# RMS norms of a two-layer encoder: column sums over dealt tokens, GpSimd's power for the inverse root, and gate rows spread by DMA

## The chip, the cores and the metric

One core of one Trainium2 chip runs the whole program in a single launch. The metric is the device time of that launch in microseconds (us), the median of the runs shown; less is better. The engines are PE (matrix products; PEld is its weight load), DVE (vector), ACT (scalar), POOL (GpSimd) and SP (here only a DMA queue). Engines run side by side and wait for each other by semaphores; each works through its own queue in order.

## The reference

A trunk of two layers on one sequence of 512 tokens, width 1024, all in float32:

```python
xn = rms_norm(x, mix_norm[layer])
# layer 0: 8 heads of forgetting attention | 4 heads of differential attention
d_out = rms_norm(d_out, subln) * 0.8            # per head and token, over 128 channels
# layer 1: mLSTM, 4 heads, 256 channels each
h = num / max(abs(den), exp(-m_t))
h = rms_norm(h, head_norm) * sigmoid(og)        # per head and token, over 256 channels
x = x + mixed @ w_out
x = x + memory_cross_attention(rms_norm(x, xattn_norm), rms_norm(mem, mem_norm), wq, wkv, wo)
x = x + conv_ffn(rms_norm(x, ffn_norm), ...)
# after both layers
return rms_norm(x, final_norm)
```

`rms_norm` is `x * rsqrt(mean(x*x) + 1e-6) * gain`. So the program needs an inverse root per token (512 numbers) in these places: the first norm of each layer, the norm ahead of each cross-attention and each FFN, the norm of the memory (256 tokens), one norm for each of the 4 differential heads and each of the 4 mLSTM heads, and the last norm.

## The kernel before, in words

**Layout.** Activations lie with channels on partitions and tokens along the free dimension: `x[k]` is 128 channels by 512 tokens, eight of them. A norm thus has to sum squares across partitions, which PE does, and has to bring the inverse root, a number per token, to all partitions, since the projections are left unnormed and each result is multiplied by `rb` (128 x 512, all rows alike) when it leaves PSUM. Every float32 operand of a projection is split in a high part (ACT copy) and a low part (DVE subtraction), and PE makes three products of them (`mm3`, L340 to L342).

**Two ways to norm.** `p_norm` (L420) sums by columns: `rsqrt_cols` (L531) makes 4 products, each with a 128-token block of the squares as weights and two columns of ones as the moving operand, so that token t of block j stands in partition t, column j. `rsqrt` (L539) then takes the inverse root of this 128 x 4 tile with 12 small DVE instructions (a first guess by integer arithmetic and three Newton steps). `bcast_cols` (L554) turns the numbers back into rows: split in two parts, each part multiplied on DVE with an identity into a 128 x 512 matrix (`sqt`), each of which PE sums with a matrix of ones (L571); the sum of the two is `rb`, in PSUM or copied to SBUF by ACT. The products of `bcast_cols` are issued at once behind its DVE work. `p_row_norm` (L433) sums by rows: the squares are split (ACT and DVE), PE multiplies both parts with ones (L470), ACT copies one row to SBUF, a DMA on ACT's queue turns the row into a 128 x 4 tile `z`, POOL takes the power -0.5 (L482), one DMA on POOL's queue writes it to DRAM (`roots`, L484) and another reads it back into all 128 partitions (L489). Its last step is tied, by `nc.vector.follow()`, behind the DVE instruction issued before it.

**Who uses which.** `p_row_norm` serves the four differential heads (tile `hrb`) and the norm ahead of each cross-attention (`x_row_norm`). `p_norm` serves the start of layer 1, the memory's norm and the four mLSTM heads, which multiply straight from PSUM (`scaled`, in `mix1`), so that a PSUM bank of the pair "s" stays taken until then. Layer 0's first norm (`inverse`, `spread` in `mix0`) and the FFN's (`root`, `spread` in `ffn_steps`) are written out, and `finish` calls `rsqrt_cols` for each half of the tokens.

**mLSTM gates.** `gates` (in `mix1`) makes rows of 4 heads x 512 tokens: `mx`, a running maximum, and `mt`. `split_rows` puts their parts in a 128 x 512 tile. For each head `most` and `emts` bring one row to all partitions: DVE makes a selector, PE multiplies (L733), and ACT copies `mxb` or takes exp(-mt) into `emt`. POOL masks `mxb` into `mk` (L1721) four times for each head, ACT takes its exponential, and DVE multiplies the scores with it.

**What orders the work.** In `mix0`, `mix1` and `xattn` a planner (`Plan`, L84) emits the steps. Each has a priority, dependencies, resources (two "s" banks, two "w" banks, four accumulators, three weight slots), a duration on PE and a `chain`: the time that other engines need until its result is ready ("A", "D", "G" for ACT, DVE, POOL; "-" for a plain delay such as a DMA). The planner keeps a clock of its own and takes the first step that would be ready at it; a step whose result is thought to be later is emitted later. The engines' queues then follow what was emitted, with shifts that the tile framework makes where no order is fixed. The FFN has a second planner (`Sched`) with its own costs for each engine; there the order on DVE and ACT is as planned.

Of the kernel before, what the change touches and what calls it, by code (L numbers as in the profile page):

```python
# [16 lines left out]
P = 128  # L17
# [13 lines left out]
ROW_DMA, SPREAD_DMA = 2.7, 6.0  # L31
# [257 lines left out]
class Builder:  # L289
# [130 lines left out]
    def p_norm(self, pl, state, n, done, scale, eps, fin, deps=(), prio=None, after=0.0, fdeps=(), chain=(("A", 0.5),)):  # L420
# [12 lines left out]
    def p_row_norm(self, pl, state, scale, eps, to, fin, deps=(), prio=None, fdeps=(), chain=()):  # L433

        nc, sp = self.nc, self.sp
        st = {}

        def parts():
            st["p"] = self.row_parts(state["sq"])

        def sums():
            st["row"] = self.row_sums(st["p"], scale, eps)

        def turned():
            st["z"] = self.row_turned(st["row"])

        def spread():
            st["rb"] = self.row_spread(st["d"], to)

        a = pl.add(parts, 0, deps, prio, chain=(("A", 0.52), ("D", 0.6)))  # L450
        a = pl.add(sums, 0.43, [a], prio, take=("s",), free=("s",), chain=(("A", 0.5),))
        a = pl.add(turned, 0, [a], prio, chain=(("-", ROW_DMA),))
        a = pl.add(lambda: st.update(d=self.row_root(st["z"])), 0, [a], prio, chain=(("G", 1.05), ("-", ROW_DMA)))
        a = pl.add(spread, 0, [a], prio, chain=(("-", SPREAD_DMA),))
# [7 lines left out]
    def row_parts(self, sq):  # L462
        hi, lo = (self.til(self.sp, "sqt", dtype=F32R) for _ in range(2))
        self.split(hi[:], lo[:], sq[:])
        return hi, lo

    def row_sums(self, parts, scale, eps):
        ps = self.bank("b")
        for i, part in enumerate(parts):
            self.nc.tensor.matmul(banked(ps[:]), self.onesr[:], alternate(part[:]), start=i == 0, stop=i == 1)  # L470
        row = self.til(self.sp, "sqt")
        self.nc.scalar.activation(folded(row[0:1, :]), restored(ps[0:1, :]), AF.Copy, scale=float(scale), bias=float(eps))
        return row

    def row_turned(self, row):
        z = self.til(self.sp, "z", (P, 4))
        self.nc.scalar.dma_start(z[:], row[0:1, :].rearrange("o (p j) -> o p j", j=4))
        return z

    def row_root(self, z):  # L480
        y = self.til(self.sp, "y", (P, 4))
        self.nc.gpsimd.tensor_tensor(out=y[:], in0=z[:], in1=self.power[:], op=ALU.pow)  # L482
        d = self.til(self.dp, "roots", (1, SEQ))
        self.nc.gpsimd.dma_start(d[:].rearrange("o (p j) -> (o p) j", j=4), y[:])  # L484
        return d

    def row_spread(self, d, to):
        rb = self.til(*to)
        self.nc.gpsimd.dma_start(rb[:], d[0:1, :].to_broadcast([P, SEQ]))  # L489
        return rb  # L490

# [5 lines left out]

    def rb_to(self):
# [1483 lines left out]
```

## Time and profile before

| what | value |
|---|---|
| median of 3 runs (lowest, highest) | 1439.73 us (1436.8, 1440.22) |
| the profiled execution | 1440.03 us, its span 1438.3 us |
| PE, PEld busy | 1411.4 us (98%), 1261.0 us (88%) |
| DVE, ACT, POOL busy | 1163.3, 817.1, 81.3 us |
| chain that ended last | PE 75%, DVE 13%, ACT 4%, DMA 4%, issue 4%, POOL 1% |
| layer 0: mixer, cross-attention, FFN | about 0 to 260, 260 to 400, 400 to 735 us |
| layer 1: mixer, cross-attention, FFN with the last norm | about 735 to 955, 955 to 1100, 1100 to 1438 us |

How to read it: the span is the time from the first to the last instruction of the profiled execution, and the run's time is a little longer. Busy time of PE is the union of its matmuls as the profile models them. A dense product of 512 columns starts every 0.21 to 0.22 us, though its record is 0.38 us long, so PE can be "busy" and still start less often than it could. In a timeline the columns are start, duration, engine, line, operation, tile written, tiles read and count; a bracket gives the idle time of that engine just before, and what ended it.

### The profile page before, as it was taken

Reading aid. Unit: us, or ns where it says so; the run is one execution under the profiler, and the core shown is the slowest. Engines: PE = TensorE matmul, PEld = TensorE weight load, DVE = VectorE, ACT = ScalarE, POOL = GpSimd, SP = SyncE. Lnnn points to the kernel's source line nnn. Section 1 sums busy time; section 2 is a strip of 40 time slices with the busy share of each in tenths; the row PEclk is TensorE's granted clock in tenths of the full one; section 3 lists DMA queues with packets and bytes.
Section 4 is the critical chain, followed back from the end, with each engine's and each line's share of the span. In section 5 each row is a group of like instructions: output and inputs, shape, how many; then the busy total and the mean of one; then the engine's idle time right before and its main releaser. Section 6 shows DMA issues by size and latency. Waiting matters only on the chain.

```text
span 1438.3 us, 22036 instructions
## 1 busy us (share of the span) xinstructions
PE 1411.4 (98%) x8304; PEld 1261.0 (88%) x8304; DVE 1163.3 (81%) x2084; ACT 817.1 (57%) x1407; POOL 81.3 (6%) x129
## 2 busy tenths in 40 slices
PE   9999799999999999999999999999999999999998
PEld 7888688889888999999888788788988899999987
DVE  7777796566689999999778858657567999999985
ACT  7777574444465556565546635444445666656654
POOL 0002230000000000000000100000000000000000
PEclk9999999999999999999999999999999999999999
DMA  5232433423237666652232222333324656555412
GB/s 202 89 96 89 118 98 131 125 88 132 87 111 205 172 159 169 162 147 78 81 103 88 90 86 90 101 105 112 129 75 134 178 161 161 165 154 169 125 60 80
DMA packets 63498, 176.36 MB, mean 123 GB/s; under 512 B 8056, under 2 KB 8056, under 8 KB 63392
## 3 DMA queue, kind: packets, MB, share of 16 engines
q1 hardware_dynamic: 55344, 152.69, 32.1%
q0 software_dynamic: 6176, 21.14, 8.1%
q8 instruction: 65, 1.06, 0.3%
q10 hardware_dynamic: 1872, 1.13, 0.3%
q14 instruction: 41, 0.34, 0.1%
HBM read 172.80 MB, written 2.13 MB: 122 GB/s over the span
## 4 chain that ended last, share of the span: by engine, by line
PE 75%; DVE 13%; ACT 4%; DMA 4%; issue 4%; POOL 1%; DVEq 0%; SPq 0%; ACTq 0%; POOLq 0%
PE acc L340 15%; PE acc L341 15%; PE acc L342 15%; PE w L342 5%; PE w L341 5%; PE w L340 5%; DVE wl L262 3%; PE s L340 2%; PE s L342 2%; PE s L341 2%; PE acc L402 2%; DVE c L262 1%; PE acc L404 1%; PE acc L403 1%; DVE x L262 1%
## 5 line engine op out<-in xcount | busy, mean ns | idle before, releaser
L262 ACT CAST wh<-raw 128x1024 fp32r<-128x1024 f32 (+2 forms) x200 | 204.2, 1023 | 200.6 <-PE acc L341 112.9
L340 PE MATMUL acc<-xh,wh 128*128 128x512 f32 (+1 forms) x824 | 289.1, 351 | 1.3 <-DVE tmp L262 1.3
L342 PE MATMUL acc<-xh,wl 128*128 128x512 f32 (+1 forms) x824 | 285.0, 346 | 0.7 <-DVE wl L262 0.7
L341 PE MATMUL acc<-xl,wh 128*128 128x512 f32 (+1 forms) x824 | 285.0, 346 | 0.0
L262 DVE TENSOR_TENSOR wl<-raw,wh 128x1024 fp32r<-128x1024 f32 (+2 forms) x200 | 238.9, 1195 | 50.2 <-ACT wh L262 49.0
L340 PEld LDWEIGHTS acc<-xh,wh 128*128 128x128 f32 x824 | 156.7, 190 | 16.5 <-issue 2.3
L342 PEld LDWEIGHTS acc<-xh,wl 128*128 128x128 f32 x824 | 156.5, 190 | 16.4 <-DVE wl L262 1.5
L341 PEld LDWEIGHTS acc<-xl,wh 128*128 128x128 f32 x824 | 156.7, 190 | 14.5 <-issue 0.2
L262 DVE SCALAR_TENSOR_TENSOR c<-hs,vec,c 128x512 f32<-128x512 f32 x176 | 131.6, 748 | 3.5 <-ACT c L262 0.6
L342 PE MATMUL w<-ah,wl 128*128 128x512 f32 x304 | 115.4, 380 | 0.2
L340 PE MATMUL w<-ah,wh 128*128 128x512 f32 x304 | 115.4, 380 | 0.0
L341 PE MATMUL w<-al,wh 128*128 128x512 f32 x304 | 115.2, 379 | 0.0
L262 ACT ACTIVATE c<-hs,vec 128x512 f32<-128x512 f32 x88 | 71.0, 810 | 26.7 <-DVE hs L262 22.5
L262 ACT CAST ah<-c 128x512 fp32r<-128x512 f32 x44 | 27.3, 620 | 89.4 <-DVE c L262 89.4
L262 DVE TENSOR_TENSOR x<-acc,x 128x512 f32<-128x512 f32 (+1 forms) x43 | 28.1, 654 | 52.6 <-PE acc L342 52.5
L342 PEld LDWEIGHTS w<-ah,wl 128*128 128x128 f32 x304 | 57.5, 189 | 9.1 <-DVE wl L262 1.0
L341 PEld LDWEIGHTS w<-al,wh 128*128 128x128 f32 x304 | 57.6, 190 | 6.6
L340 PEld LDWEIGHTS w<-ah,wh 128*128 128x128 f32 x304 | 57.6, 190 | 6.5
L340 PE MATMUL acc<-mem,wh 128*128 128x256 f32 (+1 forms) x192 | 60.7, 316 | 0.0
L342 PE MATMUL acc<-mem,wl 128*128 128x256 f32 (+1 forms) x192 | 59.9, 312 | 0.0
L341 PE MATMUL acc<-mem,wh 128*128 128x256 f32 (+1 forms) x192 | 59.6, 310 | 0.0
L1483 POOL DMA_DIRECT2D sa<-in_up_dram x33 | 28.5, 863 | 513.8 <-DVE sa L262 134.1
(357 smaller groups left out, 3729.4 us busy)
## 6 DMA issues: line engine op xcount, KB each, us to landing
raw<-in_up_dram SPq DMA_DIRECT2D x55, 512.0 KB, 3.3
sa<-in_up_dram SPq DMA_DIRECT2D x33, 512.0 KB, 4.5
sa<-in_up_dram POOLq DMA_DIRECT2D x33, 512.0 KB, 5.4
dr<-in_down_dram SPq DMA_DIRECT2D x64, 256.0 KB, 3.8
ra<-in_up_dram SPq DMA_DIRECT2D x33, 256.0 KB, 4.0
raw<-in_xk_dram SPq DMA_DIRECT2D x16, 512.0 KB, 3.3
raw<-in_wo_dram SPq DMA_DIRECT2D x16, 512.0 KB, 3.2
raw<-in_xq_dram SPq DMA_DIRECT2D x16, 512.0 KB, 3.2
```

The lines of the kernel that those rows point to most:

```text
L262: i = issue(*a, **k)
L340: mm(out, wh, xh, start=first, stop=False, skip_group_check=parts)
L341: mm(out, wh, xl, start=False, stop=False, skip_group_check=parts)
L342: mm(out, wl, xh, start=False, stop=last, skip_group_check=parts)
L402: mm(ps, xh[k][:, ts], wh, start=(k == 0), stop=False)
L403: mm(ps, xh[k][:, ts], wl, start=False, stop=False)
L404: mm(ps, xl[k][:, ts], wh, start=False, stop=(k == 7))
L1483: return add("POOL", 0.0029 * cols, lambda: nc.gpsimd.dma_start(out(), src(), accum_op=ALU.add), deps, due, (), (), 6.0)
```

## The change

Five parts.

1. **The root.** `rsqrt` takes the power -0.5 on GpSimd, one instruction, in place of 11 of its 12 DVE instructions. This holds for every norm that goes through it, the last one too.
2. **The way back.** `bcast_cols` is cut in two: `diag_cols` (split and the two DVE matrices) and `spread_cols` (the two products and the copy to SBUF). They are steps of their own in the plan, with the DVE time between them told to the planner; the same in layer 0's first norm and in the FFN's `Sched`.
3. **Far norms.** `p_row_norm` goes. `p_far_norm` serves the four differential heads and mLSTM heads 0 to 2: `rsqrt_cols`, the power on GpSimd, a write to DRAM and a read to all partitions, both DMAs on POOL's queue. The planner is told `LATE` = 12.0 us for the last DMA in place of 6.0. So that the 128 x 4 tile goes to DRAM in one piece, the squares are written dealt: `by_fours` writes token 4p+j to column 128j+p. mLSTM head 3 keeps the way over PE, by way of a tile `hrb`.
4. **Cross-attention.** Its norm goes by `p_norm`; the `follow` in `query` goes too.
5. **Gate rows.** exp(-mt) is taken once, on the rows of all heads; `mx` and exp(-mt) are written to DRAM by two DMAs, and heads 1 to 3 read their row of each to all partitions by DMA (`both`), once the queries of the head before have been evacuated; `mxb` and `emt` have two buffers in place of one. Head 0 keeps `most` and `emts`.

```diff
-ROW_DMA, SPREAD_DMA = 2.7, 6.0
+ROW_DMA, SPREAD_DMA, LATE = 2.7, 6.0, 12.0
...
         def two():
-            fin(st["r"], self.bcast_cols(st["r"], n, *done))
-
-        a = pl.add(one, 0.4 * n / 512, deps, prio, take=("s",), free=("s",), chain=(("D", 2.3),), after=after)
-        return pl.add(two, 0.5 * n / 512, [a, *fdeps], prio, take=("s",), free=("s",), chain=chain)
+            fin(st["r"], self.spread_cols(st["d"], n, *done))
+
+        a = pl.add(one, 0.9 * n / 512, deps, prio, take=("s",), free=("s",), chain=(("D", 0.1), ("G", 1.05)), after=after)
+        b = pl.add(lambda: st.update(d=self.diag_cols(st["r"], n)), 0, [a], prio, chain=(("D", 0.2 + 1.2 * n / 512),))
+        return pl.add(two, 0.43 * n / 512, [b], prio, take=("s",), free=("s",), chain=(("A", 0.5),))
+
+    def by_fours(self, to, v, **k):
+
+        self.nc.scalar.activation(to.rearrange("p (j t) -> p t j", j=4), v.rearrange("p (t j) -> p t j", j=4), AF.Square, **k)
...
+    def p_far_norm(self, pl, state, scale, eps, to, fin, deps=(), prio=None, fdeps=(), chain=(), late=None):
...
         def sums():
-            st["row"] = self.row_sums(st["p"], scale, eps)
+            st["y"] = self.rsqrt_cols(state["sq"], SEQ, scale, eps)
+
+        def away():
+            st["d"] = self.til(self.dp, "roots", (1, SEQ))
+            nc.gpsimd.dma_start(st["d"][:].rearrange("o (p j) -> (o p) j", j=4), st["y"])
 
         def spread():
-            st["rb"] = self.row_spread(st["d"], to)
+            st["rb"] = self.til(*to)
+            nc.gpsimd.dma_start(st["rb"][:], st["d"][0:1, :].to_broadcast([P, SEQ]))
+
+        a = pl.add(sums, 0.45, deps, prio, take=("s",), free=("s",), chain=(("D", 0.1), ("G", 1.05)))
+        a = pl.add(away, 0, [a], prio, chain=(("-", ROW_DMA),))
+        a = pl.add(spread, 0, [a], prio, chain=(("-", late or SPREAD_DMA),))
 
         def last():
             nc.vector.follow()
...
         nc.vector.tensor_scalar(out=z, in0=ps[:, 0 : 2 * nt : 2], scalar1=float(scale), scalar2=float(eps), op0=ALU.mult, op1=ALU.add)
-        nc.vector.tensor_scalar(out=y.bitcast(I32), in0=z.bitcast(I32), scalar1=-0.5, scalar2=1597463007.0, op0=ALU.mult, op1=ALU.add)
-        nc.vector.tensor_scalar(out=zh, in0=z, scalar1=-0.5, scalar2=None, op0=ALU.mult)
-        for _ in range(3):
-            nc.vector.tensor_tensor(out=a, in0=y, in1=y, op=ALU.mult)
-            nc.vector.tensor_tensor(out=a, in0=a, in1=zh, op=ALU.mult)
-            nc.vector.scalar_tensor_tensor(out=y, in0=a, scalar=1.5, in1=y, op0=ALU.add, op1=ALU.mult)
+        nc.gpsimd.tensor_tensor(out=y, in0=z, in1=self.power[:, :nt], op=ALU.pow)
         return y
...
                     nc.scalar.copy(o["o"][:], ps[:])
-                    nc.scalar.activation(sq["sq"][:], o["o"][:], AF.Square)
+                    self.by_fours(sq["sq"][:], o["o"][:])
...
-                f = self.p_row_norm(pl, sq, 1.0 / P, EPS, (mp, "hrb", (P, SEQ), F32, 1), scaled, [w], p + SOFT_PRIO, chain=(("D", 0.66),))
+                f = self.p_far_norm(pl, sq, 1.0 / P, EPS, (mp, "hrb", (P, SEQ), F32, 1), scaled, [w], p + SOFT_PRIO, chain=(("D", 0.66),), late=LATE)
...
-            norm = self.x_row_norm(pl, 0, self.xdone[7])
+            norm = self.x_norm(pl, 0, deps=self.xdone[7])
...
                 gt["rows"] = self.split_rows(mp, mx, mt)
+                nc.scalar.activation(mt, mt, AF.Exp, scale=-1.0)
                 gt["u"] = zi
+                gt["d"] = [self.til(self.dp, n, (H, SEQ), bufs=1) for n in ("mx", "emt")]
+                for d, v in zip(gt["d"], (mx, mt)):
+                    nc.gpsimd.dma_start(d[:], v)
...
+                def both(h=h, st=st):
+                    for i, n in enumerate(("mxb", "emt")):
+                        st[n] = self.til(mp, n, bufs=2)
+                        self.spread_row(gt["d"][i], h, st[n])
+
+                if h == 0:
+                    b1 = pl.add(most, MM, [uc, qe], p, take=("s",), free=("s",), chain=(("A", 0.5),))
+                    b2 = pl.add(emts, MM, [uc, qe], p + 1, take=("s",), free=("s",), chain=(("A", 0.5),))
+                else:
+                    b1 = b2 = pl.add(both, 0, [uc, gk, *turn[-1:]], p, chain=(("-", SPREAD_DMA),))
+                turn.append(qe)
...
-                f = self.p_norm(pl, st, SEQ, (), 1.0 / 256, 0.0, scaled, ns, p + 3, fdeps=oe, chain=(("D", 1.32),))
+                if h < 3:
+                    f = self.p_far_norm(pl, st, 1.0 / 256, 0.0, (mp, "hrb", (P, SEQ), F32, 1), scaled, ns, p + 3, fdeps=oe, chain=(("D", 1.32),), late=LATE)
+                else:
+                    f = self.p_norm(pl, st, SEQ, (mp, "hrb", 1), 1.0 / 256, 0.0, lambda r, rb, st=st: st.update(rb=rb), ns, p + 3)
+                    f = pl.add(lambda scaled=scaled, st=st: scaled(st["rb"]), 0, [f, *oe], p + 3, chain=(("D", 1.32),))
```

More of the change, by code (lines that the diff above doesn't have):

```diff
@@ L460, in p_row_norm @@
         return pl.add(last, 0, [a, *fdeps], prio, chain=chain)
[L462 to L490, printed above, removed]
     def x_norm(self, pl, prio=0, after=0.0, deps=()):
@@ L561, in bcast_cols @@
         self.sub(rl, r, rh)
-        ps = self.bank("b")
-        for i, part in enumerate((rh, rl)):
+        out = []
+        for part in (rh, rl):
             dg = self.til(self.sp, "sqt", dtype=F32R)[:].rearrange("p (a b) -> p a b", b=P)
@@ L570, in bcast_cols, with spread_cols @@
             )
-            nc.tensor.matmul(banked(ps[:, :n]), self.onesr[:], alternate(dg[:, :nt, :].rearrange("p a b -> p (a b)")), start=i == 0, stop=i == 1)
-        if pool is None:
-            return restored(ps[:, :n])
+            out.append(dg[:, :nt, :].rearrange("p a b -> p (a b)"))
+        return out
+    def spread_cols(self, diags, n, pool, tag, bufs=2):
+        ps = self.bank("b")
+        for i, dg in enumerate(diags):
+            self.nc.tensor.matmul(banked(ps[:, :n]), self.onesr[:], alternate(dg), start=i == 0, stop=i == 1)
         out = self.til(pool, tag, (P, n), bufs=bufs)
-        nc.scalar.copy(folded(out[:, :n]), restored(ps[:, :n]))
+        self.nc.scalar.copy(folded(out[:, :n]), restored(ps[:, :n]))
         return out
```

83 lines of the change are left out of this document (36 added, 47 removed).

## The prediction

> **What bounds the kernel now.** First the page's busy times, then stretches of equal kind, then what PE waits for.
>
> ```profile
> PE 1411.4 (98%) x8304; PEld 1261.0 (88%) x8304; DVE 1163.3 (81%) x2084; ACT 817.1 (57%) x1407; POOL 81.3 (6%) x129
> ```
>
> PE is idle for 1438.3 - 1411.4 = 26.9 us of the span. Everything else has room, so only two things move the end: PE's own work, and the moments in which PE waits.
>
> ```profile
> 150.00:180.00 30.00, 22.47 (x110) 17.79 (x110) 22.46 (x59) 16.37 (x33) 8.99 (x14) 0.96 0.45 123
> 300.00:400.00 100.00, 100.00 (x550) 89.82 (x549) 64.41 (x113) 47.00 (x87) 0.14 (x2) 1.00 0.30 102
> 800.00:960.00 160.00, 158.71 (x777) 134.63 (x777) 113.00 (x211) 75.64 (x112) 7.21 (x11) 1.00 0.27 93
> ```
>
> These rows of busy time by stretch give length, PE, PEld, DVE, ACT, POOL, then the granted clock. A dense stretch (300 to 400) has no idle PE; the mLSTM stretch (800 to 960) has 1.3 us. The 30 us around 165 have 7.5 us, and there the granted clock falls to 0.96. So the mLSTM part can gain little by waits, only by work; layer 0's attention can gain by waits. PE's waits over the whole span, in total, times and longest:
>
> ```profile
> PE w L1047 <- ACT pt L262: 4.6, 1, 4.6
> PE s L793 <- ACT sqt L262: 3.0, 1, 3.0
> PE s L571 <- DVE sqt L262: 2.0, 5, 0.9
> ...
> PE acc L340 <- DVE tmp L262: 1.3, 2, 0.8
> ...
> PE acc L342 <- DVE wl L262: 0.7, 2, 0.4
> ```
>
> All five lie at norms. The first two are 7.5 us of the 26.9, and both belong to the last differential head:
>
> ```profile
> 152.49 0.62 ACT L262 CAST sqt<-tb 128x512 fp32r<-128x512 f32 x1
> 157.99 0.59 PE L470 MATMUL s<-sqt,ones 128*128 128x512 f32 x2
> 161.67 0.59 ACT L262 ACTIVATE sqt<-s 1x512 f32<-1x512 f32 x1
> 162.31 0.38 PE L793 MATMUL s<-ka,qa 128*128 128x256 f32 x1 [2.97 <-ACT sqt L262]
> 169.81 0.54 POOL L489 DMA_DIRECT2D hrb<-roots  x1 [2.86 <-DMA roots<-y]
> 175.00 0.75 DVE L262 SCALAR_TENSOR_TENSOR ta<-ta,warm,hrb 128x512 f32<-128x512 f32 x1 [4.49 <-DMA hrb<-roots]
> 177.78 2.61 PE L1047 MATMUL w<-pt,v 128*64 128x512 f32 x8 [4.56 <-ACT pt L262]
> ```
>
> Read it downwards. The row sum is made at 157.99, but ACT, which is behind, copies it only at 161.67; until then an "s" bank is taken and the next scores wait 2.97 us. The row then goes through three DMAs. DVE has reached the multiplication with `hrb` in its queue and stands there for 4.49 us; ACT and the transposed weights `pt` stand behind it, and PE waits 4.56 us. The planner thought the rows would be there: its chain (1.1 + 0.9 + 2.7 + 1.1 + 2.7 + 6.0) is about 15 us, while from the split at 152.49 to 175.00 it took 22.5.
>
> **The change, part by part.** What PE pays for the two ways to sum:
>
> ```profile
> 265.37 0.59 PE L470 MATMUL s<-sqt,ones 128*128 128x512 f32 x2
> 265.80 0.38 PE L340 MATMUL acc<-xh,wh 128*128 128x512 f32 x1
> 266.02 0.38 PE L341 MATMUL acc<-xl,wh 128*128 128x512 f32 x1
> ...
> 802.86 0.95 PE L536 MATMUL s<-ones,hsq 128*128 128x2 f32 x8
> 803.67 0.46 PE L340 MATMUL acc<-xh,wh 128*128 128x512 f32 x1
> ```
>
> From start to start, two products over 512 columns take 265.80 - 265.37 = 0.43 us (0.22 each), and the column sums, eight short records with eight weight loads, 803.67 - 802.86 = 0.81.
>
> *Work of PE.* Each differential head changes row sums for column sums: 4 x (0.81 - 0.43) = +1.5. Each cross-attention norm does that and adds the two products of `spread_cols`: 2 x 0.81 = +1.6. mLSTM heads 0 to 2 lose those two products: -3 x 0.43 = -1.3. Gate rows of heads 1 to 3 lose the products of L733, two a head: -6 x 0.22 = -1.3. Together +0.5 us: as work the change is neutral.
>
> *Waits at the differential heads.* The split, the row's copy on ACT and the turning DMA go; DVE frees the bank with one instruction of 0.16 us (`z`, quoted below) instead of ACT with 0.59. So the 2.97 us go by construction, unless DVE is as late as ACT was. For the second wait the real time from the sums to `hrb` is to be compared with the planned one. Landing times and the power:
>
> ```profile
> hrb<-roots POOLq DMA_DIRECT2D x4, 256.0 KB, 4.2
> ...
> roots<-y POOLq DMA_DIRECT2D x6, 2.0 KB, 2.7
> ```
>
> ```profile
> L482 POOL TENSOR_TENSOR y<-z,power x6: 1035/1294/2126, 112.5 to 965.5; 128x4 f32<-128x4 f32 x6
> ```
>
> 0.8 (sums) + 0.2 + 1.3 (power) + 0.3 + 2.7 + 4.2 is about 9.5 us; the plan now assumes 0.45 + 0.1 + 1.05 + 2.7 + 12.0, some 16.5. DVE should meet `hrb` with up to 7 us in hand, where it was 4.5 short. Of the 7.5 us I take 6.0: without them DVE's 22.46 us of work in that stretch would have 22.5 us, so something smaller on DVE will be late next. Bounds: 0 (rival B) and 7.5. The clock comes back with it: 30 us at 0.96 cost at most 1.2; I take 0.5.
>
> *Cross-attention.* The norm came by DMA and was the last thing to arrive:
>
> ```profile
> 279.89 0.69 DVE L262 SCALAR_TENSOR_TENSOR tmp<-acc,rb 128x512 f32<-128x512 f32 x1 [5.10 <-DMA rb<-roots]
> 280.72 0.45 PE L340 MATMUL acc<-xh,wh 128*128 128x512 f32 x1 [0.51 <-DVE tmp L262]
> ```
>
> PE had filled most of the gap with keys and values, so DVE's 5.10 us of waiting cost PE only 0.51 here; over both layers 1.3 (`tmp`) and 0.7 (`wl`, the split queued behind it). By PE the rows are there some 5 us after the sums. Of these 2.0 I take 1.5, bounds 0 and 2.0, against +1.6 of work: nothing is won.
>
> *The other norms.* PE's five waits at L571 (2.0 us) come from products queued right behind their DVE work. Now that work is a planned step and PE has others in between; I take 1.6, since the last mLSTM head has little else left. The root itself, where nothing covers it, at the very end:
>
> ```profile
> 1430.14 0.16 DVE L262 TENSOR_SCALAR z<-s 128x2 f32<-128x2 f32 x1 [0.76 <-PE s L536]
> ...
> 1432.36 1.27 ACT L262 ACTIVATE th<-acc,y 128x512 f32<-128x512 f32 x2 [1.06 <-DVE y L262]
> ```
>
> From the end of `z` (1430.30) to ACT's start 2.06 us; with the power at its least (1.04, DVE having nothing else) and 0.3 to hand over, 1.35: -0.7. With the longest power (2.13) it would be +0.4.
>
> Such a long one stands here:
>
> ```profile
> 117.27 1.23 DVE L262 TENSOR_TENSOR wl<-raw,wh 128x1024 fp32r<-128x1024 f32 x1 [0.78 <-ACT wh L262]
> 117.27 2.13 POOL L482 TENSOR_TENSOR y<-z,power 128x4 f32<-128x4 f32 x1 [0.36 <-ACT wh L262]
> ```
>
> The power took 1.09 us longer than the least while DVE ran 1.23. The Trainium skill, SBUF — State Buffer, "Who interferes with whom", states that GpSimd shares a port pair with DVE as an exclusive lock: a DVE instruction with two SBUF inputs and a GpSimd one that reads SBUF don't overlap, and the second to start waits for the whole of the first. This row agrees; by that rule every power beside a busy DVE is a long one and the roots save no time against 2 us of Newton steps, which would put the sum at about 1431.
>
> *The rows of the mLSTM gates, and what the trace doesn't show.*
>
> ```profile
> 25.30 0.59 ACT L262 COPY rb<-s 128x512 f32<-128x512 f32 x1
> ...
> 104.03 0.63 ACT L262 ACTIVATE tb<-ta 128x512 f32<-128x512 f32 x1
> 114.33 0.60 POOL L484 DMA_DIRECT2D roots<-y  x1 [0.30 <-POOL y L482]
> ...
> 765.67 1.28 ACT L262 ACT_TABLE_LOAD   x1
> 770.91 0.56 ACT L262 COPY mxb<-s 128x512 f32<-128x512 f32 x1
> ```
>
> ACT is spared two copies of about 0.6 us a head, DVE two selectors; added are one exponential on four rows, two DMAs of one-off rows, and six spreads of the `hrb` kind (4.2 us to land), asked for a head ahead. Hidden by PE's projections unless POOL holds them up (rival C). The dealt write of `by_fours` is not in the trace. The plain Square (`tb`) takes 0.63; thirteen of them (4 + 3 x 3), at nothing more or at double, are 0 to 8.2 us of ACT, which is 57% busy, so 0 to +4 on the path. I take 0, since the `rb` copies, rearranged on both sides, take no longer than a Square. A moved table load is bounded by one more of 1.28; I take 0.
>
> **Sum** against the profiled execution, 1440.03: work +0.5; differential waits -6.0; clock -0.5; cross-attention -1.5; L571 -1.6; the end -0.7. That is -9.8, so 1430.2. The median of the runs lies 0.3 below that execution: **1430.0 us**.
>
> **The rivals.**
>
> *B: the waits at the differential heads stay* (chance 0.16). The column sums keep the squares' tile `tb` until PE reads it, and the fox heads' masks need the same two buffers; and a POOL that waits for `roots` (2.86 us above) still holds their masks. For it: DVE, 75% busy there with the stall in it, has no slack without it. Against: 7 us in hand. Then 6.5 us of the gain fail: 1436.5.
>
> *C: slower, by POOL's queue in the mLSTM heads* (chance 0.12). A far head puts on POOL a power (1.0 to 2.1), a write (0.6), a wait for its landing (2.2 to 2.9) and a read (0.55), 4.5 to 6.2 us in order; a gate-row read can also wait there, for a buffer of the head before last. The masks of the next head queue behind. Before, masks come this long after the sums:
>
> ```profile
> 816.28 3.08 POOL L1721 TENSOR_SCALAR_AFFINE_SELECT mk<-mxb 128x512 f32<-128x512 f32 x2 [3.46 <-ACT mxb L262]
> 825.34 0.95 PE L536 MATMUL s<-ones,hsq 128*128 128x2 f32 x8
> 841.07 1.66 POOL L1721 TENSOR_SCALAR_AFFINE_SELECT mk<-mxb 128x256 f32<-128x256 f32 x2 [19.92 <-ACT wh L262]
> 859.91 0.95 PE L536 MATMUL s<-ones,hsq 128*128 128x2 f32 x8
> 872.75 1.25 POOL L1721 TENSOR_SCALAR_AFFINE_SELECT mk<-mxb 128x512 f32<-128x512 f32 x2 [3.90 <-ACT mxb L262]
> ```
>
> 13.4 us (802.86 to 816.28), 15.7 and 12.8: more than twice 6.2, which speaks against it. It decides if masks come due within about 6 us of the sums. With three heads at some 5 us, 1430 + 15 = 1445; it is slower than before from two heads on.
>
> *D: more goes than I count* (chance 0.10). DVE loses 11 small instructions at every root and ACT two 0.6 us steps at seven heads; if smaller waits in layer 0 go too and all 7.5 are won: 7.5 + 1.2 + 2.0 + 2.0 + 0.7 - 0.5, and 3 more: 1424.
>
> **How the numbers follow.** The forecast has 0.62, its own range is 1426 to 1434 (the stated bounds of waits and roots). Leaving out C and the lower part of D, 1423.5 to 1438.5 holds about 0.8. A measurement of this kernel tells about 0.3% from no change, 4.3 us, so "faster" is below 1435.4: forecast and D, 0.72; same: B, 0.16; slower: C, 0.12.
>
> **What would show it.** Right: no wait of PE on `sqt` or `pt` of several us between 150 and 180, and PE's idle time there under 2 us at a clock of 1.00; no DVE wait of 5 us on `rb` in either cross-attention; L571 without its five waits; the last ACT writes some 0.7 us sooner after `z`. Wrong: DVE still waiting for `hrb`; PE waiting for `mk` or for scores between 780 and 900, with POOL's masks late behind a DMA; Squares of over 0.8 us on ACT.

## The result and the profile after

| | median of the runs (lowest to highest) | profiled execution's span |
|---|---|---|
| before | 1439.89 us (1436.8 to 1440.22) | 1438.3 us |
| after | 1431.96 us (1431.57 to 1432.4) | 1429.8 us |

The ratio after to before is 0.995, 95% interval 0.9933 to 0.9967: faster by 0.5%. The forecast was 1430.0, the span fell by 8.5 us where the sum had 9.8. The total is near; the stages are not, and that is what the experiments are about.

To see the stages, take the start of the column sums ahead of each FFN, at the start of layer 1 and at the end as marks. Every kernel of this study has these marks, with the same sums at them, so the lengths between them can be compared. Each length is of one profiled execution; the runs of the kernel before lie up to 3.4 us apart, those of the change 0.8. (The sums ahead of the cross-attentions are no such mark: by rows they begin only behind a split, by columns at once.)

| from the start to ... / length of | before | after | difference |
|---|---|---|---|
| FFN sums of layer 0 (mixer, cross-attention) | 406.24 | 401.84 | -4.40 |
| FFN of layer 0 | 330.00 | 330.45 | +0.45 |
| mixer and cross-attention of layer 1 | 364.81 | 360.63 | -4.18 |
| FFN of layer 1 | 321.78 | 322.21 | +0.43 |
| last sums to the end | 15.47 | 14.67 | -0.80 |
| span | 1438.3 | 1429.8 | -8.5 |

The first and the third length can be cut once more, at the last addition to the squares ahead of the cross-attention. Behind it PE makes the same products in both kernels, but for the norm's own. The first two lines are of before, the others of after:

```profile
262.16 0.69 DVE L262 TENSOR_TENSOR sq<-sq,sqt 128x512 f32<-128x512 f32 x1
956.69 0.69 DVE L262 TENSOR_TENSOR sq<-sq,sqt 128x512 f32<-128x512 f32 x1
```

```profile
259.22 0.69 DVE L262 TENSOR_TENSOR sq<-sq,sqt 128x512 f32<-128x512 f32 x1
950.31 0.69 DVE L262 TENSOR_TENSOR sq<-sq,sqt 128x512 f32<-128x512 f32 x1
```

Layer 0's mixer thus lost 262.16 - 259.22 = 2.9 us and its cross-attention 1.5; layer 1's mixer lost 2.4 (220.45 to 218.02) and its cross-attention 1.8 (144.36 to 142.61).

The busy line of the page after, to be held against that of before:

```profile
PE 1410.2 (99%) x8332; PEld 1262.6 (88%) x8332; DVE 1142.1 (80%) x1953; ACT 814.2 (57%) x1393; POOL 98.5 (7%) x150
```

PE's busy time is the same within 1.2 us; its idle time fell from 26.9 to 1429.8 - 1410.2 = 19.6 us. DVE lost 21 us of busy time and POOL gained 17, and neither shows in the span as such. The busy times by stretch (length, PE, PEld, DVE, ACT, POOL, granted clock):

```profile
150.00:180.00 30.00, 27.73 (x149) 23.14 (x148) 17.87 (x41) 13.33 (x26) 7.25 (x12) 0.94 0.30 89
800.00:960.00 160.00, 159.49 (x785) 135.75 (x784) 101.27 (x149) 74.48 (x105) 14.77 (x22) 1.00 0.31 101
```

The 30 us around 165 have 27.7 us of PE in place of 22.5, and a granted clock of 0.94 where it was 0.96. These two are means and mislead. Between 10 us and the last 20 us the clock is 1.00 in both kernels but for one stretch at 0.50, 3.41 us long. The first row is of before, the second of after:

```profile
177.64:181.05 3.41, 3.27 (x11) 1.86 (x12) 2.66 (x10) 0.09 (x1) 0.00 (x0) 0.50 0.25 84
```

```profile
155.94:159.35 3.41, 3.41 (x10) 2.68 (x9) 2.60 (x5) 2.44 (x6) 2.00 (x4) 0.50 0.29 78
```

Before, the window's end at 180 cuts off a part of that stretch. So the clock costs the same in both, at most half of 3.41, 1.7 us of PE's work. What PE waits for, in total, times and longest:

```profile
PE w L781 <- DVE pt L262: 2.3, 1, 2.3
PE s L1705 <- ACT k L262: 1.8, 2, 0.9
PE s L1614 <- DVE cv L262: 1.5, 1, 1.5
...
PE s L534 <- DVE sqt L262: 0.2, 1, 0.2
```

The waits of 4.6 and 3.0 us at the last differential head are gone, and so are those of `tmp` and nearly all behind `sqt` (2.0 to 0.2). In the mLSTM two waits have grown: L1614's on `cv` to 1.5 us from 0.6, and the one ahead of the products of `q` and `k` (L1705) to 1.8 from 0.8. One new wait stands at the top, on `pt`. It lies at the differential heads again:

```profile
142.52 0.95 PE L499 MATMUL s<-ones,tb 128*128 128x2 f32 x8
143.59 1.23 DVE L262 TENSOR_TENSOR wl<-raw,wh 128x1024 fp32r<-128x1024 f32 x1
143.75 1.95 POOL L507 TENSOR_TENSOR y<-z,power 128x4 f32<-128x4 f32 x1 [2.54 <-DVE z L262]
146.00 0.61 POOL L448 DMA_DIRECT2D roots<-y  x1 [0.30 <-POOL y L507]
148.40 1.12 ACT L262 ACTIVATE tb<-ta 128x512 f32<-128x512 f32 x1
148.77 0.55 POOL L452 DMA_DIRECT2D hrb<-roots  x1 [2.16 <-DMA roots<-y]
152.17 0.75 DVE L262 SCALAR_TENSOR_TENSOR ta<-ta,warm,hrb 128x512 f32<-128x512 f32 x1 [1.72 <-DMA hrb<-roots]
155.23 0.44 PE L781 MATMUL w<-ident,x 128*128 128x128 f32 x2 [2.27 <-DVE pt L262]
```

This is head 2. From the sums to the multiplication it took 152.17 - 142.52 = 9.65 us, and the forecast had worked out 9.5. But DVE had reached that multiplication at 152.17 - 1.72 = 150.45, only 7.9 us after the sums, not the 16.3 that the planner was told in all (the prediction adds it up to 16.5). The masking, the softmax and the copies of `pt` behind it on DVE are late by these 1.72 us, and PE waits 2.27. About 0.9 us of the chain is what the power took longer, 1.95 us here and 1.03 at the next head.

The DMAs of the far norms, their median times from issue to landing, and the powers:

```profile
hrb<-roots POOLq DMA_DIRECT2D x7, 256.0 KB, 3.8
...
roots<-y POOLq DMA_DIRECT2D x7, 2.0 KB, 2.0
```

```profile
L507 POOL TENSOR_TENSOR y<-z,power 128x4 f32<-128x4 f32 x14 | 18.5, 1320 | 287.9 <-DVE z L262 287.8
...
L507 POOL TENSOR_TENSOR y<-z,power 128x2 f32<-128x2 f32 x3 | 2.1, 709 | 104.1 <-DVE z L262 104.1
```

The landings are shorter than the forecast took them (4.2 and 2.7), and the power of 128 x 4 has the 1.3 that it took. The cross-attention, and the end, where the last root has no cover:

```profile
259.96 1.05 PE L499 MATMUL s<-ones,sq 128*128 128x2 f32 x8
266.77 0.59 ACT L262 COPY rb<-s 128x512 f32<-128x512 f32 x1 [3.49 <-PE s L534]
267.39 1.37 DVE L262 SCALAR_TENSOR_TENSOR tmp<-acc,rb 128x512 f32<-128x512 f32 x2 [2.32 <-ACT rb L262]
...
1422.51 0.16 DVE L262 TENSOR_SCALAR z<-s 128x2 f32<-128x2 f32 x1 [0.76 <-PE s L499]
1422.82 0.70 POOL L507 TENSOR_TENSOR y<-z,power 128x2 f32<-128x2 f32 x1 [6.11 <-DVE z L262]
1423.56 1.27 ACT L262 ACTIVATE th<-acc,y 128x512 f32<-128x512 f32 x2
```

DVE's wait for `rb` fell from 5.10 to 2.32 us, and PE has none behind it. At the end ACT starts 1423.56 - 1422.67 = 0.89 us after `z`, where it was 2.06.

### The profile page after: what moved, and what is told of

Its sections match the earlier page's. It is cut to its first block, busy times and chain, and to the rows that moved or that the text cites. A ratio compares the mean times of both kernels' runs of the same rounds, so it can differ in the third digit from the quotient of the medians.

```text
span 1429.8 us, 21962 instructions
## 1 busy us (share of the span) xinstructions
PE 1410.2 (99%) x8332; PEld 1262.6 (88%) x8332; DVE 1142.1 (80%) x1953; ACT 814.2 (57%) x1393; POOL 98.5 (7%) x150
## 3 DMA queue, kind: packets, MB, share of 16 engines
q8 instruction: 65, 1.06, 0.3%
q10 hardware_dynamic: 1008, 1.12, 0.2%
## 4 chain that ended last, share of the span: by engine, by line
PE 78%; DVE 11%; ACT 5%; issue 4%; DMA 1%; POOL 1%; POOLq 0%; SPq 0%; DVEq 0%; ACTq 0%
PE acc L340 15%; PE acc L341 15%; PE acc L342 15%; PE w L342 5%; PE w L340 5%; PE w L341 5%; DVE wl L262 3%; PE s L340 2%; PE s L342 2%; PE s L341 2%; PE acc L402 2%; PE acc L404 2%; PE acc L403 2%; DVE x L262 2%; PE w L1749 1%
```

## The experiments

All are the changed kernel with one edit, unless said otherwise. Times are medians of the runs; "stages" are the five lengths of the table above (after: 401.84, 330.45, 360.63, 322.21, 14.67). Kernels whose code for layer 0 is the changed kernel's own reach the first mark between 401.84 and 403.56, with the wait on `pt` between 2.3 and 3.0 us; so in that stage a difference of under 2 us says nothing by itself. The clock is a part of this: it stands at 0.50 for 3.41 us there in the change and for 6.83 us in run 8, which has the 403.56. Between kernels with the same FFN its length agrees within 0.2 us in layer 0 and within 0.5 in layer 1.

**1. The planner told 6.0 us, as before the change (late6).**

```diff
-ROW_DMA, SPREAD_DMA, LATE = 2.7, 6.0, 12.0
+ROW_DMA, SPREAD_DMA, LATE = 2.7, 6.0, 6.0
```

> The changed kernel with LATE = 6.0 in place of 12.0, so that the planner takes the last DMA of a far norm for as short as before. Theory (the time told to the planner): from the column sums to the rows it takes 9.7 us, the plan would think about 10.5, DVE meets hrb too early again, waits of 3 us and more on it come back at the differential heads, and the time is 1434 to 1437 us. Rival (the shorter chain alone, three DMAs to two and no copy on ACT): the rows are there within the 10.5 us, no such wait, 1431 to 1433 us.

Measured: 1426.72 us (1426.3 to 1427.31), ratio to before 0.9913 (0.9899 to 0.9928). Both theories fall: telling the planner a later arrival is not what saves the time, it costs 4.3 us in the spans and 5.2 in the medians. The stages are 397.57, 330.40, 360.71, 322.21, 14.61, so all of it lies in layer 0. Sums of heads 2 and 3, and the multiplication of head 2:

```profile
137.91 0.95 PE L499 MATMUL s<-ones,tb 128*128 128x2 f32 x8
146.23 0.98 PE L499 MATMUL s<-ones,tb 128*128 128x2 f32 x8
...
155.40 0.74 DVE L262 SCALAR_TENSOR_TENSOR ta<-ta,warm,hrb 128x512 f32<-128x512 f32 x1
```

```profile
150.00:180.00 30.00, 29.83 (x169) 25.38 (x169) 26.48 (x65) 18.76 (x41) 7.99 (x15) 1.00 0.36 115
```

Heads 2 and 3 come 4.6 and 5.8 us sooner (142.52 and 152.01 in the change), DVE meets `hrb` without a wait, and the stretch has a full clock and 26.5 us of DVE work in place of 17.9. The 3.41 us at half clock are gone too; they can be up to 1.7 of the 4.3 us.

**2. The kernel before, told 12.0 for its differential heads (before_late12).**

```diff
-f = self.p_row_norm(..., scaled, [w], p + SOFT_PRIO, chain=(("D", 0.66),))
+f = self.p_row_norm(..., scaled, [w], p + SOFT_PRIO, chain=(("D", 0.66),), late=12.0)
```

> The kernel before with one number changed: the planner is told 12.0 us for the last DMA of the four differential heads' row norms in place of 6.0; the sums stay by rows. Theory (the time told to the planner): PE's wait of 4.6 us behind hrb goes, the 3.0 us in which ACT has not copied the row stay, 1434 to 1437 us. Rival (the shorter chain): with 22.5 us from split to rows against 21 planned the wait stays, 1439 to 1441 us.

Measured: 1435.72 us (1433.33 to 1436.47), ratio 0.9974 (0.9964 to 0.9983); the expected 1434 to 1437. The wait of 4.6 us on `pt` is gone; the first mark stands at 402.76. The clock still has its 3.41 us at 0.50, from 160.33 on. There 12.0 helped: the way by rows really took 22.5 us and 15 had been told. So the same number is good for the long chain and bad for the short one.

**3. What 12.0 costs the short chain: a third buffer (nta3).**

```diff
-            NTA = 2
+            NTA = 3
```

> The changed kernel, LATE still 12.0, with three buffers for the differential heads' outputs (tile ta) in place of two. Theory: what LATE = 12.0 costs is this: the planner gives a buffer free only when the row norm of the head before last is planned as done, so head 2 may not be weighed until the late step of head 0 has passed; head 2's sums stand at 142.5 us where they stood at 137.9 with 6.0, and PE runs out of other work at 152. With a third buffer the sums of heads 2 and 3 come at about 138 and 147, no wait on pt of over 1 us follows, and the time is 1426.5 to 1428.5. Rival: the late steps themselves, wherever the heads stand, put the work in a worse order; then the wait stays and the time is 1431 to 1433.

Measured: 1429.15 us (1428.47 to 1429.48), ratio 0.9933 (0.992 to 0.9947). With LATE still 12.0 the wait on `pt` is gone and the clock is full again; the first mark stands at 399.03, 2.8 us sooner. Sums of heads 2 and 3, and the stretch:

```profile
126.71 0.95 PE L499 MATMUL s<-ones,tb 128*128 128x2 f32 x8
145.22 0.95 PE L499 MATMUL s<-ones,tb 128*128 128x2 f32 x8
```

```profile
150.00:180.00 30.00, 29.25 (x159) 24.20 (x157) 25.31 (x72) 17.00 (x37) 7.76 (x15) 1.00 0.33 110
```

So the buffer is a link in it. Head 2 can't be weighed until a `ta` is free, and the planner frees one when head 0's late step is, in its own clock, done. A longer delay told for head 0 holds back head 2, and by that head 3 and the work that would have stood beside them. The third buffer cuts that link, and half or more of late6's gain comes back (2.8 of 5.2 us in the medians, 2.8 of 4.3 in the stage; the full clock, up to 1.7 us, is in both). Head 2 came 11 us sooner than expected, though, and the time is above the expected 1426.5 to 1428.5: the order is a third one, and the rest stays open.

**4. The root by Newton steps on DVE again (newton).** The planner is told 2.3 us of DVE in place of POOL's 1.05.

```diff
-nc.gpsimd.tensor_tensor(out=y, in0=z, in1=self.power[:, :nt], op=ALU.pow)
+nc.vector.tensor_scalar(out=y.bitcast(I32), in0=z.bitcast(I32), scalar1=-0.5, scalar2=1597463007.0, op0=ALU.mult, op1=ALU.add)
+nc.vector.tensor_scalar(out=zh, in0=z, scalar1=-0.5, scalar2=None, op0=ALU.mult)
+for _ in range(3):
...
```

> The changed kernel with the root by 12 DVE instructions again, the plan told 2.3 us. Theory: the power is worth only what it saves at the very end, 0.9 us, against about 0.4 us that each FFN loses by it (sums to spread 6.1 us against 5.2): 1431.5 to 1433, with the last stage 0.9 us longer. Rival: the DVE time that the power frees is what lets the differential heads keep their slack: waits on hrb or pt of over 1 us more between 140 and 180, and 1434 or more.

Measured: 1436.1 us (1433.64 to 1436.98), ratio 0.9973 (0.9963 to 0.9982). Stages 405.36, 330.31, 361.34, 322.04, 15.45. Each theory has its part: the end is longer by 0.78 us, and the FFNs are shorter by 0.14 and 0.17, which lies within the scatter named above; and layer 0 is longer by 1.8 us or more than the band above, as the rival had it, with one wait that the change doesn't have:

```profile
PE w L1015 <- ACT pt L262: 3.7, 1, 3.7
```

Where it comes from is to be seen at head 3, whose sums stand at 156.14 in this run:

```profile
161.16 0.15 DVE L262 TENSOR_SCALAR z<-s 128x4 f32<-128x4 f32 x1
168.09 0.16 DVE L262 SCALAR_TENSOR_TENSOR y<-a,y 128x4 f32<-128x4 f32 x1
175.18 0.75 DVE L262 SCALAR_TENSOR_TENSOR ta<-ta,warm,hrb 128x512 f32<-128x512 f32 x1 [4.35 <-DMA hrb<-roots]
```

The first and the last of the 12 small instructions stand 6.9 us apart, since other DVE work is queued between them, and DVE then waits 4.35 us for `hrb` (3.26 at head 2). The power is slower than it need be beside DVE (1.32 us in the mean, 1.01 at its least), but it is one instruction on an idle engine. How much of the longer stage the order of the plan has in it, this run doesn't separate.

**5. The Squares plain, the weights taken in steps (weights_dealt).** The dealing moved from the Square's output to PE's weight load.

```diff
-self.nc.tensor.matmul(ps[:, 2 * t : 2 * t + 2], sq[:, t * P : (t + 1) * P], ...)
+w = sq[:].rearrange("p (t j) -> p j t", j=4)[:, t, :] if dealt else sq[:, t * P : (t + 1) * P]
+self.nc.tensor.matmul(ps[:, 2 * t : 2 * t + 2], w, ...)
```

> The changed kernel with the dealing moved from the Square to the column sums: the Squares of the far norms are written in order (0.63 us in the trace of before, 1.14 dealt), and PE takes each block of weights with a step of four tokens. 13 Squares of 0.5 us less on ACT, 6.6 us. Theory (ACT stands on the path at the differential heads, where PE waits 2.3 us behind pt): 1428 to 1430.5 us. Rival (ACT at 57% covers it): 1431 to 1433 us. If a stepped weight load costs PE time, the column sums take more than 0.81 us from start to start.

Measured: 1437.31 us (1434.71 to 1438.4), ratio 0.9986 (0.9976 to 0.9995). The warning in the expectation came true. All sums of the differential heads as a group, 32 products:

```profile
L500 PE MATMUL s<-ones,tb 128*128 128x2 f32 x32 | 7.4, 352 | 0.0
```

```profile
L499 PE MATMUL s<-ones,tb 128*128 128x2 f32 x32 | 3.8, 241 | 0.0
```

The first row is this kernel, the second the change: 7.4 us of PE for four heads in place of 3.8, so 0.9 a head and 6.3 for seven, all on the engine that bounds. The first stage grew by 4.6 (four heads), the mLSTM by 2.3 (three).

**6. The Squares plain, the dealing done by the write to DRAM (dealt_by_dma).**

```diff
-nc.gpsimd.dma_start(st["d"][:].rearrange("o (p j) -> (o p) j", j=4), st["y"])
+nc.gpsimd.dma_start(st["d"][:].rearrange("o (j p) -> (o p) j", p=P), st["y"])
```

> The changed kernel with plain Squares (0.63 us in place of 1.14), the dealing done by the write to DRAM instead: 512 pieces of 4 bytes to their places in token order. The sums and the weights' layout stay as they are. Theory: ACT's 13 times 0.5 us lie off the path, and the longer write is covered by the slack of about 7 us: 1431 to 1433. Rival: the longer Squares are what the stage of the differential heads pays for, so 1428 to 1430. Should the write land more than 4 us later than 2.7, DVE will wait for hrb again and the time goes above 1433.

Measured: 1471.0 us (1469.38 to 1471.96), ratio 1.0214 (1.019 to 1.0237). The write's landing, DVE's wait and PE's behind it:

```profile
roots<-y POOLq DMA_DIRECT2D x7, 2.0 KB, 9.6
```

```profile
139.27 0.75 DVE L262 SCALAR_TENSOR_TENSOR ta<-ta,warm,hrb 128x512 f32<-128x512 f32 x1 [9.16 <-DMA hrb<-roots]
142.84 0.58 PE L750 MATMUL s<-ka,qa 128*128 128x256 f32 x1 [11.14 <-ACT ka L262]
```

2 KB in 512 pieces of 4 bytes land after 9.6 us, in 16-byte pieces after 2.0. Layer 0 pays 21 us for it and the mLSTM 19 (380.0 for 360.6). The clock stands at 0.50 for 23.9 us in layer 0 and 17.1 us in the mLSTM, up to 12 and 8.5 us of these prices. So the slack of the chain ends somewhere below 7.6 us more, and past it the price is steep. What PE's 11 us wait for is DVE's own wait for `hrb`, not masks behind POOL's DMAs.

**7. The dealt Square written in the order of its output (dealt_read).**

```diff
-to.rearrange("p (j t) -> p t j", j=4), v.rearrange("p (t j) -> p t j", j=4)
+to.rearrange("p (j t) -> p j t", j=4), v.rearrange("p (t j) -> p j t", j=4)
```

> The changed kernel with the same dealt layout of the squares, but the Square written in the order of its output (it reads every fourth number and writes in one piece, where the change reads in one piece and writes 512 bytes apart). First question: the Square's duration, 1.14 us in the change, 0.63 for a plain one. If it comes down to about 0.7: by the theory that these 13 Squares lie off the path the time stays at 1431 to 1433; by the rival that ACT's 0.5 us a piece delays the heads it is 1428 to 1430. If it stays at 1.1, the reads cost what the writes did and nothing changes.

Measured: 1432.41 us (1432.17 to 1433.65), ratio 0.9958 (0.9944 to 0.9971). The Square got no shorter but longer. Its four executions at the differential heads, in this kernel and in the change (busy, mean ns of one):

```profile
L262 ACT ACTIVATE tb<-ta 128x512 f32<-128x512 f32 x4 | 5.5, 1383 | 0.2
```

```profile
L262 ACT ACTIVATE tb<-ta 128x512 f32<-128x512 f32 x4 | 4.5, 1122 | 0.2
```

The stages do not follow it: 402.86 lies inside the band of layer 0, the mLSTM took 360.27. Another 0.26 us a piece is not to be seen, so the 0.5 us that the dealing costs is at least not paid in full on the path; how much a plain one would bring couldn't be told, since both ways to have it cost more elsewhere.

**8. The first three mLSTM heads by way of PE (mlstm_near).** The Squares there are plain then; the gate rows stay with the DMAs.

```diff
-                if h < 3:
+                if h < 0:
                     f = self.p_far_norm(...)
```

> The changed kernel with mLSTM heads 0 to 2 normed over PE like head 3 (hrb by spread_cols, plain Squares). Theory (only PE's work counts there): 6 products of 0.22 us come back, 1432.5 to 1434 us. Rival (DMAs on POOL's queue cost something there that hides part of the gain): 1429 to 1431.5 us.

Measured: 1432.54 us (1431.82 to 1433.47), ratio 0.9954 (0.9939 to 0.9969). The mLSTM stage is 360.98 against 360.63: the far norms are worth 0.35 us there, not the 1.3 of six products spared. Even the 0.35 is small beside the scatter: kernels with the change's code for this stage take 360.38 (run 12) to 360.71 (run 1).

**9. The gate rows of all heads by way of PE (gate_pe).** The exponential on four rows and the two DMAs behind it go too; far norms stay.

```diff
-                if h == 0:
+                if True:
                     b1 = pl.add(most, ...)
                     b2 = pl.add(emts, ...)
```

> The changed kernel with the gate rows of all four mLSTM heads over PE, as before (selectors, products, copies), the far norms kept. Theory: the rows by DMA save what PE is spared, 6 products of 0.22 us, and nothing else, since ACT and DVE have room: 1433 to 1434, all of it between 750 and 950. Rival: the spared ACT copies and DVE selectors count as well, or PE waited for the rows: 1434.5 or more. Second rival: the six reads from DRAM slow the weight streams as much as they spare: 1431 to 1432.5.

Measured: 1438.66 us (1436.36 to 1440.56), ratio 0.9996 (0.9985 to 1.0007): the change's gain is gone. The mLSTM stage is 366.79, 6.2 us more than in the change. At head 1:

```profile
813.00 0.59 ACT L262 COPY mxb<-s 128x512 f32<-128x512 f32 x1
...
820.81 1.06 ACT L262 ACTIVATE th<-num 128x512 f32<-128x512 f32 x1
821.90 0.69 DVE L262 TENSOR_TENSOR hsq<-hsq,th 128x512 f32<-128x512 f32 x1 [0.70 <-ACT th L262]
822.65 1.87 PE L499 MATMUL s<-ones,hsq 128*128 128x2 f32 x8 [3.94 <-DVE hsq L262]
```

Here ACT is the one that is late: it copies `mxb`, takes `emt`, and the long dealt Squares `th` are behind that in its queue. PE waits 3.94 us for the last sum of squares. From 822.32 on the clock is at 0.50 for 6.83 us, which can be up to 3.4 of the 6.2 us. ACT's average of 57% says nothing about this place.

Runs 8 and 9 make a table of four, for layer 1's mixer alone: from its first sums to the last addition to the squares.

| layer 1's mixer, us | gate rows by PE | gate rows by DMA |
|---|---|---|
| norms over PE | 220.4 (before) | 218.4 (run 8) |
| far norms | 224.2 (run 9) | 218.0 (after) |

The gate rows by DMA are the gain, 2.1 us or 6.2; the far norms alone would lose 3.7. The kernel before also has the Newton steps and the undivided way back in its cell: in run 4 the Newton steps made this mixer 0.7 us longer, so the 2.1 is not the gate rows' alone for certain.

**10. The cross-attention's norm by rows again (xattn_row).** `p_row_norm` as in the kernel before, for the cross-attentions only.

```diff
-            norm = self.x_norm(pl, 0, deps=self.xdone[7])
+            norm = self.x_row_norm(pl, 0, self.xdone[7])
...
+                        if h == 0:
+                            nc.vector.follow()
```

> The changed kernel with the norm ahead of each cross-attention by rows again (split, two products, three DMAs, and the tie in the queries). Theory of the prediction: 1.6 us of PE work saved against 1.5 us of waits that come back, so 1431 to 1433, the changed kernel's own time. Rival, from the stage marks (the cross-attentions take 141.9 and 141.9 us from norm to FFN sums in the changed kernel, 140.9 and 141.2 before): the way over PE costs 0.7 to 1.0 us each, so 1429.5 to 1430.8, with the 0.5 us waits on tmp back and still a shorter stage.

Measured: 1434.92 us (1432.22 to 1435.85), ratio 0.9964 (0.9952 to 0.9976). Neither theory held: the way over PE saves time. From the last addition to the squares to the FFN's sums, layer 0 takes 142.62 us in the change and 144.45 here, layer 1 142.61 and 143.31: 1.8 and 0.7 us. (Every other kernel with sums by columns takes 142.60 to 142.62 in both layers.) The waits are back:

```profile
277.84 0.69 DVE L262 SCALAR_TENSOR_TENSOR tmp<-acc,rb 128x512 f32<-128x512 f32 x1 [5.48 <-DMA rb<-roots]
278.68 0.46 PE L340 MATMUL acc<-xh,wh 128*128 128x512 f32 x1 [0.89 <-DVE tmp L262]
```

The idle time in a bracket is not the whole price of such a wait. In the kernel before, the product ahead of the wait of 0.51 us at 280.72 is this one:

```profile
279.83 0.38 PE L404 MATMUL acc<-wh,mem 128*128 128x512 f32 x1
```

The next starts 0.89 us later, where dense products start 0.22 apart: 0.67 us of starts are lost, while the record, 0.38 long, leaves only 0.51 idle. Behind its norm the kernel before has four such waits in each cross-attention (0.51, 0.37, 0.39 and 0.11 us; 0.79, 0.37, 0.39 and 0.12), and the change has none. From start to start they come to about 2.3 and 2.6 us; less 0.8 for the added products, that is 1.5 and 1.8, and the stages gained 1.5 and 1.8.

The rival of this run had compared the sums' starts, which is a wrong mark: by rows the squares are split first, so the sums begin later, and the stage seems shorter by what has moved ahead of the mark.

**11. LATE = 6.0 with the Square of run 7 (late6_read).**

```diff
-ROW_DMA, SPREAD_DMA, LATE = 2.7, 6.0, 12.0
+ROW_DMA, SPREAD_DMA, LATE = 2.7, 6.0, 6.0
...
-to.rearrange("p (j t) -> p t j", j=4), v.rearrange("p (t j) -> p t j", j=4)
+to.rearrange("p (j t) -> p j t", j=4), v.rearrange("p (t j) -> p j t", j=4)
```

> The changed kernel with LATE = 6.0 and the Square written in the order of its output: the two edits together, as a candidate for the best. If the Squares lie off the path, the time of LATE = 6.0 alone, 1426 to 1427.5; if they are on it, 1423 to 1425.5.

Measured: 1426.98 us (1426.63 to 1427.8), ratio 0.9919 (0.9906 to 0.9933): the same as LATE = 6.0 alone, as for Squares off the path.

**12. LATE = 6.0 with the FFN's norm as before (late6_ffn).**

```diff
-                self.r = self.rsqrt(n["ps"], 4, 1.0 / DM, EPS)
+                self.r = self.rsqrt_newton(n["ps"], 4, 1.0 / DM, EPS)
...
-            b = add("DVE", 0.2, root, [a], a.prio, (), [("s", st)])
-            b = add("POOL", 1.05, None, [b], a.prio)
-            b = add("DVE", 1.6, diag, [b], a.prio)
+            b = add("DVE", 2.1, root, [a], a.prio, (), [("s", st)])
```

The diagonals are made in `spread` again, right ahead of the products.

> The changed kernel with LATE = 6.0 and the FFN's norm as before the change (Newton steps on DVE, the two products queued at once behind the diagonals), as a candidate for the best. The two FFN stages, from their sums to the next mark, took 330.0 and 321.8 us before and 330.4 and 322.2 in the changed kernel. Theory: the 0.4 us each are the later arrival of rb (6.1 us after the sums against 5.2) and come back, so 0.8 us less than LATE = 6.0 alone: about 1425.9, at the stages 330.0 and 321.8. Rival: with the 12 DVE instructions and the five waits behind the diagonals back, nothing is won: 1426.5 to 1427.5, at the stages 330.4 and 322.2.

Measured: 1425.84 us (1425.27 to 1426.88), ratio 0.9909 (0.9892 to 0.9925), the fastest of this study and faster than both kernels. The FFN stages are 329.95 and 321.69 against 330.40 and 322.21: 0.45 and 0.52 us back. Its sums and the first of the two products, and below the same in the change:

```profile
396.59 0.95 PE L1333 MATMUL s<-ones,sq 128*128 128x2 f32 x8
...
401.78 0.48 PE L549 MATMUL s<-sqt,ones 128*128 128x512 f32 x1 [0.26 <-DVE sqt L262]
```

```profile
401.84 0.95 PE L1318 MATMUL s<-ones,sq 128*128 128x2 f32 x8
...
407.91 0.59 PE L534 MATMUL s<-sqt,ones 128*128 128x512 f32 x2
```

PE waits 0.26 us for the diagonal in the one and not at all in the other, and yet the one with the wait is quicker: the products stand 5.2 us behind the sums in place of 6.1. Newton steps alone (run 4) gave back 0.14 to 0.17 of it at most, so most of the 0.45 seems to come from the step of its own, for which the FFN's planner is told 1.05 + 1.6 us.

## Why the prediction was right, and where it was not

The time, 1431.96, is inside the range and near the forecast by luck in part: errors of opposite sign nearly cancel. Here the sum's terms stand by place, with the -1.6 of L571 shared out by its five waits (0.89, 0.26, 0.32, 0.32, 0.26):

| place | forecast | measured |
|---|---|---|
| layer 0's mixer | -5.7 | -2.9 |
| both cross-attentions | +0.1 | -3.2 |
| both FFNs | -0.4 | +0.9 |
| layer 1's mixer | -3.1 | -2.4 |
| the end | -0.7 | -0.8 |

- **Differential heads, -6.0 of waits.** This step failed in part. The two old waits did go, and "something smaller on DVE will be late next" came as a wait of 2.27 us. What failed is "up to 7 us in hand": the real chain was as worked out (9.65 against 9.5), but the 16.3 told to the planner did not put 16.3 us of other work ahead of the multiplication; DVE was there after 7.9. A planned delay only helps if work exists to fill it, and a delay that also holds a buffer takes that work away (runs 1 and 3). With LATE = 6.0 this mixer gains 262.16 - 254.96 = 7.2 us against before, more than the 5.7, with up to 1.7 of clock in it.
- **Clock, -0.5.** It gave nothing: 3.41 us at 0.50 in both kernels. The 0.96 that the term was worked out from had caught only a part of that stretch.
- **Cross-attention, +1.6 - 1.5.** The mis-sized term is the 1.5. The waits went as forecast, but they were worth 4.9 us, not 2.0: two of the four in each layer had not been counted, and idle time between records is less than the starts that are lost (run 10). The 1.6 us of added work is there, by the same count.
- **L571, -1.6.** The waits fell by 1.8 us as forecast, but each FFN grew by 0.45 us (run 12), since `rb` comes later.
- **mLSTM, -1.3 - 1.3.** The sum is near, its parts are not. The gate rows are mis-sized, about 2.1 to 6.2 in place of 1.3; in run 9 it is ACT's queue that makes the rows by PE dear. The far norms gave 0.35 in place of 1.3, if anything, and waits on `cv` and ahead of `q` and `k` grew by 1.9.
- **The end, -0.7.** It measured -0.8, but not by the working. That had the power at 1.04 us; this one (128 x 2) took 0.70, so ACT starts 1.17 us sooner after `z`, and the other 0.4 is lost behind it.
- **`by_fours` at nothing.** The Square takes 1.12 us, near the upper bound of double (1.26), and "Squares of over 0.8 us" was a sign of being wrong. The `rb` copies were no guide: they read every second number and write in one piece. That it costs little on the path fits runs 7 and 11, as far as they go.
- **The rule on the shared port** (the Trainium skill, SBUF — State Buffer, "Who interferes with whom") would have had the roots save no time. The trace agrees with the rule: the power at 143.75 above, beside the DVE instruction with two inputs at 143.59, took 1.95 us. In the whole trace five of 14 such powers are long (1.48 to 1.95 us); each began while a DVE instruction with two inputs from SBUF ran and ended about 0.9 us after it. The other nine took 1.01 to 1.06. But run 4 is slower without the powers, so what was drawn from it for the time doesn't hold here.
- **Rivals.** B came in part, as a smaller wait with another cause. C did not come: PE has no wait of several us in the mLSTM heads, and their mixer is 2.4 us shorter. D's time needs LATE = 6.0: then 1426.7, or 1425.8 with run 12's FFN. Of the signs of being right one failed narrowly: PE is idle for 2.27 us between 150 and 180, and the clock there is not 1.00.

## What to carry to other kernels

A delay told to a planner is not slack: ask what is held while it runs (a buffer, a bank), and which work that keeps from filling it; the best number need not be the longest, nor the measured one. Judge a stage by marks that both kernels reach with the same work behind them, and undo each part of a change by itself: of this one's five parts the gate rows, the cross-attention and the last root paid, the FFN's share cost 0.9 us, and the number 12.0 cost 4 to 5. Price a wait of PE from start to start of its products, not by the idle time between records, and before a mean clock is compared look where its low stretch begins and ends. An engine at 57% can still be the one that ends last at one place, so look at the queue there before a copy is called free.

## What was not expected of the hardware

- An ACT Square of 128 x 512 takes 0.63 us, 1.12 if its output goes 512 bytes apart, and 1.12 to 1.57 if its input is read every fourth number (1.38 in the mean at the differential heads).
- Loading float32 weights from every fourth column makes eight column sums 1.82 us long instead of 0.95.
- A DMA of 2 KB lands after 2.0 us in 16-byte pieces and after 9.6 in 4-byte pieces.
- POOL's power of 128 x 4 takes 1.01 to 1.95 us in the change, that of 128 x 2 about 0.71.
- Between 10 us and the last 20 us of a span the granted clock is either 1.00 or 0.50 in all 14 traces, and each stretch at 0.50 lasts 3.41 us or twice, three or four times that (6.83, 10.24, 13.65). The change, with a wait of PE of 2.3 us, and run 2, with none over 1.8 us there, have one such stretch; runs 1 and 3, with none over 0.5 us between 140 and 180, have none.
